# Norm tails, router and the lone expert unit of a two-block network: three edits in one change

## The chip, the cores and the metric

The kernel runs on one core of one Trainium2 chip. The time is device microseconds of one execution, as the median of several; one more execution was recorded by the hardware profiler, and every row below comes from that one.

## The reference, cut to what matters

256 tokens of width 1024 (`x`, two blocks of 128 tokens) pass through two layers of a first block and one layer of a second, all in float32.

```python
for l in range(2):                                  # first block
    x = layernorm(ALPHA * x + 0.5 * swiglu(x, ffn1))          # tail 1, 4
    x = layernorm(ALPHA * x + hybrid_mixer(x))                # tail 2, 5
    x = layernorm(ALPHA * x + 0.5 * swiglu(x, ffn2))          # tail 3, 6
h = rms_norm(x) * (1 + scale1) + shift1             # second block
x = x + gate1 * (concat(gated_deltanet(h), window_attention(h)) @ w_out)   # tail 7
h2 = rms_norm(x) * (1 + scale2) + shift2
# router: best of 4 groups, two experts of its 8, by softmax of h2 @ w_group, h2 @ w_router
for e in range(32):
    out += combine[:, e] * ((silu(h2 @ w_gate[e]) * (h2 @ w_up[e])) @ w_down[e])
x = x + gate2 * out
```

An expert is three matrices of 1024 x 256, 1024 x 256 and 256 x 1024.

## The kernel before, in words

**Products.** Dense weights are loaded as tiles of 128 x 1024, and `wload` makes of each a pair `hi` (a rounded copy, ScalarE, L304) and `lo` (the rest, VectorE, L305); the activations are kept as such a pair too, transposed, in `xhl`. Each product is then three matmuls. `execute` walks a list of items and loads up to two tiles ahead. A scheduler puts the instructions of each engine into an order when the kernel is built, by program order and priority; `keep_in_program_order` fixes an instruction's place, and each engine then runs its list in that order.

**A tail.** `outp` multiplies by an output matrix (w_out of a feed-forward part, w_mix_out, w_out_2), one tile of 128 rows after another, for both token blocks `tb`. The last four tiles are kept, and all their products for block 0 are done before those for block 1, so that the norm of block 0 (`finisher`'s `fn(0)`) runs beside the products of block 1. `fn` adds the residual (L500), takes mean and variance (L501, L503), the inverse root on GpSimd (L314), scales (L508, L509); `to_T` then transposes the block on TensorE (L331) and splits it into `xhl`. In the program, `to_T` of block 0 comes behind all products of block 1, and `to_T` of block 1 at the end of `fn(1)`. The next part starts with a leading product that does block 0 first, so that the norm of block 1 runs beside it; two of its four weight tiles go to spare buffers (`SPARE`). There are five such plain tails. In the sixth, ahead of the second block, `modnorm` follows with the second block's first norm: squares on ScalarE, an inverse root, then two VectorE passes over each half with gain and shift along rows (L1275, L1277).

**The router.** After `outp` by w_out_2, `fn` multiplies by the gate and adds (L1859, L1860), transposes the block (L1869, copies L1871), multiplies by the router's weights (L1873), and `tokens` makes a pair `th`, `tl` of the normed tokens (L1933, L1935), written so that the columns of one residue modulo 8 lie together. `route` then works out both experts of each token on VectorE. `moe` starts with eight products that put `x` into the output banks (L2257).

**The experts.** 32 experts in 16 pairs, up to 64 tokens each. For a pair: `gather` multiplies a 0/1 matrix by `th`, `tl` as weights (L2245: 256 products with a weight load of 128 columns each), `hidden` (L2085), `activate`, `turn` (L2103, L2107), `down` (L2122), `scatter` (L2141). The two experts of a pair sit in columns 0 to 63 and 64 to 127 of the array. One extra unit (`extra`, between the eighth and ninth pair) takes what one expert could not hold: 64 rows, one expert, so only columns 0 to 63. Weights of experts stream in meanwhile, through 14 large and 5 small buffers.

## Time and profile before

| | |
|---|---|
| median of 3 runs | 2105.73 us (2105.18 to 2108.71) |
| profiled execution, its own time | 2107.98 us |
| its span, first to last instruction | 2106.2 us |
| busy shares of the span | TensorE 98%, its weight loads 78%, VectorE 70%, ScalarE 52%, GpSimd 4% |
| chain that ended last | TensorE 86%, VectorE 8%, ScalarE 2% |
[...]
| moved by DMA | 427.60 MB, mean 203 GB/s |

A busy share says little by itself where it is an average over many stages; what an edit is worth is read from the stretch in which it lies. In the profile PE is TensorE's matmuls, PEld its weight loads, DVE VectorE, ACT ScalarE, POOL GpSimd; L331 is line 331 of the kernel before.

### The profile page before, as it was taken

The numbers are of one execution on the slowest core, as the hardware profiler recorded it, in microseconds if no ns is written. First come the engines' busy times: TensorE is split into PE (matmuls) and PEld (weight loads), VectorE is DVE, ScalarE is ACT, GpSimd is POOL, SyncE is SP. The second block draws the span as 40 slices with busy tenths as digits, with TensorE's granted clock in tenths as the row PEclk, the third lists the DMA queues.
The fourth block names the chain that finished last, engine by engine and source line by source line (L and its number), as shares of the span: only waits on it lengthen the run. The fifth ranks groups of instructions, "written<-read, shape, count | busy, mean of one in ns | idle before, by whom it ended". The sixth has DMA issues, their size and how long they took to land.

```text
span 2106.2 us, 30863 instructions
## 1 busy us (share of the span) xinstructions
PE 2057.2 (98%) x11507; PEld 1650.7 (78%) x11507; DVE 1470.6 (70%) x2782; ACT 1105.4 (52%) x2026; POOL 75.3 (4%) x64
## 2 busy tenths in 40 slices
PE   8999999999999999999999999999998999899998
PEld 7887877888888888888877888888887878645543
DVE  6886688987878677875688896877666675533333
ACT  5654565777655544554466776754553554322222
POOL 0000000100000000000000110000000121001000
PEclk9999999999999999999999999999999989999999
DMA  7985544454659676876544355565674423799996
GB/s 229 304 261 175 166 133 135 129 162 141 192 193 303 190 256 197 273 242 205 162 123 142 109 161 169 151 224 167 188 235 137 136 63 116 265 364 357 357 374 235
DMA packets 278825, 427.60 MB, mean 203 GB/s; under 512 B 21806, under 2 KB 206352, under 8 KB 277648
## 3 DMA queue, kind: packets, MB, share of 16 engines
q1 hardware_dynamic: 278240, 422.44, 61.6%
q0 software_dynamic: 432, 3.15, 0.4%
q8 instruction: 92, 1.51, 0.3%
q14 instruction: 61, 0.50, 0.1%
HBM read 424.46 MB, written 1.07 MB: 202 GB/s over the span
## 4 chain that ended last, share of the span: by engine, by line
PE 86%; DVE 8%; ACT 2%; issue 1%; POOL 1%; DMA 0%; SPq 0%; ACTq 0%; POOLq 0%; DVEq 0%
PE ps L408 27%; PE ps L411 14%; PE ps L2085 6%; PE y L342 5%; PE y L343 5%; PE y L345 4%; PE ps L2122 3%; PE ps L342 3%; PE ps L345 3%; PE ps L343 3%; DVE lo L305 2%; PE ps L2245 2%; PE y L2141 1%; PE y L331 1%; PE ps L301 1%
## 5 line engine op out<-in xcount | busy, mean ns | idle before, releaser
L305 DVE TENSOR_TENSOR lo<-raw,hi 128x1024 fp32r<-128x1024 f32 (+1 forms) x556 | 660.2, 1196 | 250.5 <-ACT hi L304 175.0
L304 ACT CAST hi<-raw 128x1024 fp32r<-128x1024 f32 (+1 forms) x556 | 556.6, 1028 | 337.5 <-PE y L345 169.6
L408 PE MATMUL ps<-xhl,hi 128*128 128x512 f32 x2240 | 568.4, 395 | 0.8 <-DVE kc L181 0.8
L408 PEld LDWEIGHTS ps<-xhl,hi 128*128 128x128 f32 x2240 | 402.1, 189 | 76.2 <-issue 3.3
L411 PEld LDWEIGHTS ps<-xhl,lo 128*128 128x128 f32 x2240 | 306.1, 190 | 21.7
L411 PE MATMUL ps<-xhl,lo 128*128 128x256 f32 x2240 | 314.7, 283 | 0.0
L342 PE MATMUL y<-hi,hh 128*128 128x512 f32 x352 | 137.3, 390 | 0.0
L343 PE MATMUL y<-lo,hh 128*128 128x512 f32 x352 | 137.0, 389 | 0.0
L342 PE MATMUL ps<-hi,xhl 128*128 128x512 f32 (+1 forms) x304 | 121.8, 402 | 3.5 <-DVE ra L803 2.2
L2085 PE MATMUL ps<-wgu,hi 128*64 128x512 f32 x512 | 121.1, 594 | 0.0
L345 PE MATMUL ps<-hi,xhl 128*128 128x512 f32 (+1 forms) x304 | 118.7, 393 | 1.9 <-DVE xhl L305 1.9
L343 PE MATMUL ps<-lo,xhl 128*128 128x512 f32 (+1 forms) x304 | 120.1, 395 | 0.0
L179 ACT ACTIVATE ysum<-ps 128x256 f32<-128x256 f32 x168 | 64.3, 383 | 77.4 <-PE ps L411 73.4
L345 PE MATMUL y<-hi,hl 128*128 128x512 f32 x352 | 104.5, 389 | 0.0
L2085 PEld LDWEIGHTS ps<-wgu,hi 128*64 128x64 f32 x512 | 42.6, 137 | 68.2 <-issue 64.7
L181 DVE TENSOR_TENSOR ysum<-ysum,ps 128x256 f32<-128x256 f32 x168 | 69.3, 415 | 29.0 <-ACT ysum L179 28.7
L342 PEld LDWEIGHTS y<-hi,hh 128*128 128x128 f32 x352 | 66.1, 188 | 14.8 <-issue 1.2
L345 PEld LDWEIGHTS y<-hi,hl 128*128 128x128 f32 x352 | 66.1, 188 | 13.7
L343 PEld LDWEIGHTS y<-lo,hh 128*128 128x128 f32 x352 | 66.1, 188 | 13.5
L342 PEld LDWEIGHTS ps<-hi,xhl 128*128 128x128 f32 x304 | 58.2, 192 | 19.4 <-ACT qs L795 3.0
L179 ACT ACTIVATE sg<-ps 128x256 f32<-128x256 f32 x80 | 30.4, 380 | 80.5 <-PE ps L411 80.4
L345 PEld LDWEIGHTS ps<-hi,xhl 128*128 128x128 f32 x304 | 58.1, 191 | 15.8 <-DVE xhl L305 4.3
(604 smaller groups left out, 3192.8 us busy)
## 6 DMA issues: line engine op xcount, KB each, us to landing
raw<-in_w_mix_in_dram SPq DMA_DIRECT2D x184, 512.0 KB
raw<-in_ffn_w_in_dram SPq DMA_DIRECT2D x176, 512.0 KB
raw<-in_ffn_w_out_dram SPq DMA_DIRECT2D x88, 512.0 KB
wgu<-in_w_gate_dram SPq DMA_DIRECT2D x64, 512.0 KB
wgu<-in_w_up_dram SPq DMA_DIRECT2D x64, 512.0 KB
lo<-in_w_down_dram SPq DMA_DIRECT2D x54, 512.0 KB
wada<-in_w_ada_dram SPq DMA_DIRECT2D x96, 256.0 KB
raw<-in_w_branch_dram SPq DMA_DIRECT2D x48, 512.0 KB
```

The source lines that it names most:

```text
L179: self.nc.scalar.activation(out, pb, AF.Copy, scale=scale)
L181: self.nc.vector.tensor_tensor(out, out, pa, op=ALU.add)
L304: self.nc.scalar.copy(hi, src)
L305: self.nc.vector.tensor_tensor(lo, src, hi.bitcast(F32), op=ALU.subtract)
L342: mm(y, ah[:, t], wh[:, c], start=start, stop=False)
L343: mm(y, ah[:, t], wl[:, c], start=False, stop=False)
L345: mm(y, al[:, t], wh[:, c], start=False, stop=stop)
L408: mm(ps.rearrange("p (a b) -> p a b", a=2), h[:, k % 4, c], xh.both(k), start=k == 0, stop=False)
L411: mm(ps[:, 0:256], l[:, k % 4, c], xh[:, k, :], start=False, stop=k == KD - 1)
L2085: mm(gu[64 * e:64 * e + 64, c], u["x"](k)[:, 64 * e:64 * e + 64], w, start=k == 0 and i == 0, stop=k == KD - 1 and i == len(ws[0]) - 1)
L2122: mm = lambda *a, **kw: self.placed(pin, self.nc.tensor.matmul(*a, **kw))
L2245: nc.tensor.matmul(ps[:, j, :], B["t"][tb][i][:, 128 * k:128 * k + 128], P[:, tb, :], start=n == 0, stop=n == 3)
```

## The change

- **Tails.** The last 6 tiles are kept in place of 4 (8 in the sixth tail), 2 or 4 of their pairs in large buffers; up to four tiles are loaded ahead of a spare one, and a third spare one is added. Block 1's products are done by halves of the columns, and `to_T` of block 0 is put into them (`mid`, ahead of item 18 of 24, or 24 of 32). `fn` and `to_T` are given a priority; `to_T` of block 1 is put right ahead of the leading product's part for block 1 (`late`). The transposes are fixed in program order.
- **Second block's norm (sixth tail).** Only the scale by the inverse root is done along rows; gain and shift come after the transposes, as columns (`modx`), and the load of their rows is dropped. The router's constants (`head`) are worked out here, not ahead of w_out_2.
- **Router.** The transposes of block 0 go ahead of the last four items of block 1's products; the order behind is: transposes of block 1's first half, router products of block 0, transposes of its second half, its router products. `tokens` writes in natural order, and the second parts `tl` are fixed in program order. `gather` takes its weights with a step of 8 elements (32 bytes).
- **Extra unit.** Gate in columns 0 to 63 and up in 64 to 127; for the output, column half 0 in the one and half 1 in the other; in `scatter`, half 0 from rows 0 to 63 and half 1 from rows 64 to 127.

```diff
-PRIO = {'narrow': 300, 'rope2': 300}
-
-SPARE, SPARE2 = (1, 2), (1,)
+PRIO = {'narrow': 300, 'rope2': 300, 'norm': 300}
+
+SPARE, SPARE2 = {1: "s2", 2: "s2", 3: "big"}, {1: "s2", 2: "s2", 3: "own"}
...
+TAIL, TAIL_BIG, MID = (6, 8), (2, 4), (18, 24)
...
-                while nxt < len(ws) and len(loaded) <= ahead:
+                while nxt < len(ws) and len(loaded) <= (4 if ws[nxt][5] else ahead):
...
-        if spare:
+        if spare == "big":
+            t = self.big.tile([128, 2048], F32R, name="wtail", tag="b8")
+            hi, lo = (t[:, i * 1024:i * 1024 + 1024] for i in range(2))
+            self.split(hi, lo, raw)
+            return (hi.rearrange("p (a b) -> p a b", a=a), lo.rearrange("p (a b) -> p a b", a=a))
+        if spare == "s2":
...
-        self.split(hi[:, :n], lo[:, :n], raw[:, :n])
+        last = self.split(hi[:, :n], lo[:, :n], raw[:, :n])
+        if self.pin:
+
+            self.tc.keep_in_program_order(last)
...
+                            if tb == NB - 1:
+                                self.late()
...
-            self.W(w[:, kn * j:kn * j + kn, c0:c0 + n], kn, n, tile(j), lead and j in spare)
...
-                        for part in ((0,), (1,)):
-                            for i, wt in enumerate(st["w"]):
-                                one(kt - last + i, wt, tb, part)
-                        fn(tb, st["ys"][tb])
+
+                        halves = [(0,), (1,)] if mid is not None and tb == NB - 1 else [(0, 1)]
+                        for n, (c, part, i) in enumerate((c, p, i) for c in halves for p in (0, 1) for i in range(last)):
+                            if len(halves) > 1 and n == mid[0]:
+                                mid[1]()
+
+                            one(kt - last + i, st["w"][i], tb, (part,), c, len(halves) > 1 and last == 4 and n >= mid[0])
+                        with self.tc.high_priority(prio) if prio else ExitStack():
+                            fn(tb, st["ys"][tb])
...
-            self.W(w[:, order[k]:order[k] + 1, :], 1, D, tile(k))
...
-                st["m"] = self.modrows(0, 1, "gain1")
                 st["h"] = self.t8([128, NB, D], F32, "h1")
+                self.B["head"] = self.head(self.B)
+                next(self.B["head"])
...
-            src = st["h"] if mod else st["x"]
-            if tb == NB - 1:
-                self.to_T(S_, src, 0)
...
-                h = st["h"][:, tb, :]
-                self.modnorm(st["x"][:, tb, :], st["m"], lambda n, t, s: (h[:, n * 512:n * 512 + 512], t, s))
+
+                x, h = st["x"][:, tb, :], st["h"][:, tb, :]
+                r = self.modnorm1(x, [h[:, 0:512], h[:, 512:1024]])[0][:, 0:1]
+                nc.scalar.activation(h[:, 0:512], x[:, 0:512], AF.Identity, scale=r)
+                nc.vector.tensor_scalar(h[:, 512:1024], x[:, 512:1024], r, None, op0=ALU.mult)
             if tb == NB - 1:
                 S_["x"] = st["x"]
-                self.to_T(S_, src, 1)
-        return pre, fn
-
-
-    def to_T(self, S_, x, tb):
+                self.late, self.pin = late, True
+
+        def mid():
+            with self.tc.high_priority(PRIO["norm"]):
+                self.to_T(S_, st["h"] if mod else st["x"], 0, mod)
+
+        def late():
+            self.pin = False
+            if mod:
+                next(self.B["head"])
+            with self.tc.high_priority(PRIO["norm"]):
+                self.to_T(S_, st["h"] if mod else st["x"], 1, mod)
+        return pre, fn, mid
...
-            pt = self.transposes(x[:, tb, j * 512:(j + 1) * 512])
+            pt = self.transposes(x[:, tb, j * 512:(j + 1) * 512], pin=True)
             o = (slice(None), slice(4 * j, 4 * j + 4), slice(tb * 128, tb * 128 + 128))
+            if mod:
+                y = self.sc([128, 4, 128], F32, "modx", True)
+                for k in range(4):
+                    shift, gain = (self.modc[:, i + 4 * j + k:i + 4 * j + k + 1] for i in (0, 8))
+                    if j:
+                        self.nc.vector.tensor_scalar(y[:, k, :], pt[:, k, :], gain, shift, op0=ALU.mult, op1=ALU.add)
+                    else:
+                        self.nc.scalar.activation(y[:, k, :], pt[:, k, :], AF.Identity, scale=gain, bias=shift)
+                pt = y
             self.split(xh[o], xl[o], pt)
-        if tb == NB - 1:
-            S_["xT"] = (xh, xl)
+        S_["xT"] = (xh, xl)
...
                     for tb in range(NB):
-                        ps = st["ps"][tb]
                         if not first:
+                            if tb == NB - 1:
+                                self.late()
                             for i in range(4):
                                 one(i, tb)
+                    for tb in range(NB):
...
+        self.outp(lambda k: (H[k // 8][0][:, k % 8, :], H[k // 8][1][:, k % 8, :]), wout, KF, fn, last=TAIL[mod], pre=pre,
+                  big=TAIL_BIG[mod], mid=(MID[mod], mid), prio=PRIO["norm"])
...
         self.JOIN("swa")
-        self.DO(lambda: (B.update(pj=True), B["head"]()))
+        self.DO(lambda: (B.update(pj=True), next(B["head"], None)))
...
+        hT = {}
+
+        def turned(tb, j, pin=False):
+            pt = self.bank([128, 4, 128], pj=True)
+            for k in range(4):
+                t = nc.tensor.transpose(pt[:, k, :], S_["x"][:, tb, (4 * j + k) * 128:(4 * j + k + 1) * 128], self.ident)
+                if pin:
+                    self.tc.keep_in_program_order(t)
+            hT[tb, j] = self.sc([128, 4, 128], F32, "xT2")
+            nc.scalar.copy(hT[tb, j], pt)
+
+        def logits(tb, j):
+            for k in range(4 * j, 4 * j + 4):
+                nc.tensor.matmul(B["pr"][:, tb, :], hT[tb, j][:, k % 4, :], B["wr"][:, k, :], start=k == 0, stop=k == KD - 1)
+
+
+        def mid():
+            B["pr"] = self.bank([128, 2, 36], pj=True)
+            for j in range(2):
+                turned(0, j, True)
...
             if tb == 0:
-                B["pr"] = self.bank([128, 2, 36], pj=True)
+                nrm = self.modnorm1(x)
+                B["rs"].append(nrm[0][:, 0:1])
+                self.tokens(B, x, nrm[0][:, 0:1])
+                return
+            turned(1, 0)
+            logits(0, 0)
+            logits(0, 1)
+            turned(1, 1)
+            logits(1, 0)
+            logits(1, 1)
+
+            B["lo"][0]()
             nrm = self.modnorm1(x)
             B["rs"].append(nrm[0][:, 0:1])
-            hT = []
-            for j in range(2):
-                pt = self.bank([128, 4, 128], pj=True)
-                for k in range(4):
-                    nc.tensor.transpose(pt[:, k, :], x[:, (4 * j + k) * 128:(4 * j + k + 1) * 128], self.ident)
-                hT.append(self.sc([128, 4, 128], F32, "xT2"))
-                nc.scalar.copy(hT[j], pt)
-            for k in range(KD):
-                nc.tensor.matmul(B["pr"][:, tb, :], hT[k // 4][:, k % 4, :], B["wr"][:, k, :], start=k == 0, stop=k == KD - 1)
             self.tokens(B, x, nrm[0][:, 0:1])
-            if tb == 0:
-                B["lo"][0]()
-        return pre, fn, head
+        return pre, fn, mid
...
+        yield
+        ps = self.bank([128, 36], pj=True)
+        for k in range(KD):
+            self.tc.keep_in_program_order(nc.tensor.matmul(ps, self.modc[:, 24 + k:25 + k].to_broadcast([128, 128]), wr[:, k, :],
+                                                           start=k == 0, stop=k == KD - 1))
...
+        B["wr"] = self.hi_p.tile([128, 1024], F32, name="hi", tag="hi")[:, 0:KD * 36].rearrange("p (k n) -> p k n", k=KD)
+        nc.vector.tensor_tensor(B["wr"], wr, self.modc[:, 32:40].rearrange("p (k o) -> p k o", o=1).to_broadcast([128, KD, 36]), op=ALU.mult)
+        B["rs"], B["t"], B["lo"] = [], [], []
...
-        to = lambda a: a.rearrange("p (k q) -> p q k", k=KD)
-        xv = x.rearrange("p (q k) -> p q k", k=KD)
-        nc.scalar.activation(to(th), xv, AF.Identity, scale=r)
+        nc.scalar.activation(th, x, AF.Identity, scale=r)
         B["t"].append((th, tl))
-        B["lo"].append(lambda: nc.vector.scalar_tensor_tensor(to(tl), xv, r, to(th).bitcast(F32), op0=ALU.mult, op1=ALU.subtract))
+        B["lo"].append(lambda: self.tc.keep_in_program_order(
+            nc.vector.scalar_tensor_tensor(tl, x, r, th.bitcast(F32), op0=ALU.mult, op1=ALU.subtract)))
...
+            if u.get("alone"):
+
+                for i, (_, w) in enumerate(ws[0]):
+                    mm(gu[64 * i:64 * i + 64, 0:256], u["x"](k)[:, 0:64], w, start=k == 0, stop=k == KD - 1)
+                continue
...
+        if u.get("alone"):
+            nc.scalar.activation(h[0:64, :], gu[0:64, 0:256], AF.Silu)
+            nc.vector.tensor_copy(h[64:128, :], gu[64:128, 0:256])
+            u["h"] = h
+            return
...
-        nc.scalar.copy(u["hT"][:, :, 0:m], pt[:, 0:2, 0:m])
+        if u.get("alone"):
+            hT = u["hT"][:, :, 0:64]
+            nc.scalar.copy(hT, pt[:, 0:2, 0:64])
+            nc.vector.tensor_tensor(hT, hT, pt[:, 0:2, 64:128], op=ALU.mult)
...
+        if u.get("alone"):
+
+            y = self.bank([128, 512], pj=True)
+            yg, yh, yl = (self.sc([128, 512], dt, i) for dt, i in ((F32, "yg"), (F32R, "yh"), (F32R, "yl")))
+            for k in range(2):
+                for n in range(2):
+                    mm(y[64 * n:64 * n + 64, :], u["hT"][:, k, 0:64], u["wd"][0][k][:, n * 512:n * 512 + 512], start=k == 0, stop=k == 1)
+            for n in range(2):
+                q = slice(64 * n, 64 * n + 64)
+                self.nc.vector.scalar_tensor_tensor(yg[q, :], y[q, :], u["w"][q, :], B["gt"][q, 1, n * 512:n * 512 + 512], op0=ALU.mult, op1=ALU.mult)
+            self.split(yh, yl, yg)
+            u["y"] = [(yh, yl)] * 2
+            return
...
+        if u.get("alone"):
+            for tb in range(NB):
+                for i in range(2):
+                    for n in ns:
+                        q = slice(64 * n, 64 * n + 64)
+                        mm(ys[tb][n], u["PT"][q, tb, :], u["y"][n][i][q, :], start=start and i == 0, stop=stop and i == 1)
+            return
...
+        u["alone"] = m == 64
+        if u["alone"]:
+
+            for t in range(NB):
+                nc.vector.tensor_copy(Po[t][:, :, 64:128], Po[t][:, :, 0:64].bitcast(F32))
+        u["Pw"] = lambda tb: Po[tb][:, 2, 0:128 if u["alone"] else m].bitcast(F32)
...
-                nc.vector.tensor_copy(xs[n][0:m, :], ps[0:m, :])
+
+                for j in range(2):
+                    nc.vector.tensor_copy(xs[j].rearrange("s (k p) -> s k p", k=4)[0:m, :, 64 * n:64 * n + 64],
+                                          ps[0:m, :].rearrange("s (p k) -> s k p", k=KD)[:, 4 * j:4 * j + 4, :])
...
-                    nc.tensor.matmul(ps[:, j, :], B["t"][tb][i][:, 128 * k:128 * k + 128], P[:, tb, :], start=n == 0, stop=n == 3)
+                    nc.tensor.matmul(ps[:, j, :], B["t"][tb][i][:, k:D:KD], P[:, tb, :], start=n == 0, stop=n == 3)
```

## Rows read from the trace of the kernel before

**Rows 1.** Busy time by stretch: tails 1 and 5, tail 6, router; from the last product on.

```profile
core 0: us, PE busy (x) PEld busy (x) DVE busy (x) ACT busy (x) POOL busy (x), PEclk, DMA share, GB/s
200.30:216.20 15.90, 14.45 (x69) 10.75 (x67) 13.72 (x22) 6.58 (x9) 1.00 (x1) 1.00 0.47 135
...
1430.30:1447.00 16.70, 15.08 (x117) 13.66 (x116) 13.96 (x21) 7.86 (x12) 1.00 (x1) 1.00 0.45 129
1618.70:1637.10 18.40, 11.80 (x42) 8.50 (x41) 16.86 (x38) 7.14 (x16) 2.02 (x3) 0.72 0.40 120
1818.50:1838.80 20.30, 15.90 (x78) 11.57 (x76) 13.34 (x53) 8.26 (x13) 0.56 (x1) 0.75 0.76 285
```

**Rows 2.** Timeline, tail 1, TensorE: start, us, what, idle before and who ended it.

```profile
201.74 0.50 PE L342 MATMUL ps<-hi,xhl 128*128 128x512 f32 x1 [0.33 <-ACT xhl L304]
...
207.23 0.39 PE L343 MATMUL ps<-lo,xhl 128*128 128x512 f32 x1
...
207.46 0.40 PE L345 MATMUL ps<-hi,xhl 128*128 128x512 f32 x1
...
208.64 1.32 PE L331 MATMUL y<-ctab,x 128*128 128x128 f32 x8 [0.78 <-DVE x L509]
...
211.03 0.50 PE L345 MATMUL ps<-hi,xhl 128*128 128x512 f32 x1 [0.33 <-DVE xhl L305]
```

**Rows 3.** Timeline, tail 1, VectorE: first and last step of block 0's norm.

```profile
194.90 1.28 DVE L500 SCALAR_TENSOR_TENSOR x<-x,y 128x512 f32<-128x512 f32 x2 [1.88 <-PE y L345]
...
199.05 1.41 DVE L509 SCALAR_TENSOR_TENSOR x<-x,rs,lngb 128x512 f32<-128x512 f32 x2
```

**Rows 4.** Timeline, tail 6: the modulated norm and its transposes.

```profile
1621.42 1.42 DVE L1275 SCALAR_TENSOR_TENSOR mn<-x,ssm,gain 128x512 f32<-128x512 f32 x2
1622.76 1.29 DVE L1277 TENSOR_TENSOR h<-mn,gain 128x512 f32<-128x512 f32 x2
...
1623.50 1.97 PE L331 MATMUL y<-ctab,h 128*128 128x128 f32 x8 [4.60 <-DVE h L1277]
...
1635.71 1.26 PE L331 MATMUL y<-ctab,h 128*128 128x128 f32 x8 [0.72 <-DVE h L1277]
```

**Rows 5.** Timeline of the router, TensorE.

```profile
1819.84 1.98 PE L1873 MATMUL ps<-hi,xT 128*128 128x36 f32 x16 [0.29 <-ACT xT L1871]
...
1824.98 1.09 PE L1869 MATMUL ps<-ctab,x 128*128 128x128 f32 x4 [2.70 <-DVE x L1860]
1826.11 3.63 PE L1873 MATMUL ps<-hi,xT 128*128 128x36 f32 x16
...
1836.79 2.12 PE L2245 MATMUL ps<-P,raw 128*128 128x256 f32 x16 [0.90 <-DVE P L2220]
```

**Rows 6.** Timeline of the router, VectorE: the second part of block 1's tokens.

```profile
1830.56 1.97 DVE L1935 SCALAR_TENSOR_TENSOR raw<-x,ssm,raw 128x1024 fp32r<-128x1024 f32 x1
```

**Rows 7.** Groups by line and form, experts (1838 to 2100 us): busy, mean ns | idle.

```profile
L2085 PE MATMUL ps<-wgu,hi 128*64 128x512 f32 x512 | 121.1, 594 | 0.0
...
L2085 PEld LDWEIGHTS ps<-wgu,hi 128*64 128x64 f32 x512 | 42.6, 137 | 68.2 <-issue 64.7 <-DVE yg L2130 1.7 <-DVE hi L2207 0.3
L2245 PE MATMUL ps<-P,raw 128*128 128x256 f32 x248 | 33.7, 286 | 0.0
L2245 PEld LDWEIGHTS ps<-P,raw 128*128 128x128 f32 x246 | 30.3, 188 | 3.7 <-issue 2.4 <-DVE yg L2130 1.2
...
L2085 PE MATMUL ps<-wrow,hi 128*64 128x256 f32 x32 | 7.1, 379 | 0.0
...
L2122 PE MATMUL ps<-wrow,hT 128*64 128x512 f32 x8 | 3.6, 598 | 0.0
...
L2141 PE MATMUL y<-yh,PT 64*128 64x512 f32 x4 | 1.7, 416 | 0.0
```

**Rows 8.** Single lines: duration ns min/median/max, first and last start, forms.

```profile
L1933 ACT ACTIVATE raw<-x,ssm x2: 2052/2067/2082, 1820.2 to 1826.6; 128x1024 fp32r<-128x1024 f32 x2
...
L304 ACT CAST hi<-raw x556: 292/1049/1102, 9.4 to 1801.8; 128x1024 fp32r<-128x1024 f32 x176, 128x512 fp32r<-128x512 f32 x9, 128x128 fp32r<-128x128 f32 x1
...
L2107 PEld LDWEIGHTS y<-ctab,hs x34: 195/200/220, 1857.7 to 2090.0; 128*128 128x128 f32 x32, 64*128 64x128 f32 x2
```

**Rows 9.** Busy time by stretch, experts; columns as in the first group.

```profile
2000.00:2010.00 10.00, 10.00 (x49) 3.19 (x46) 2.79 (x4) 1.24 (x2) 0.00 (x0) 1.00 0.68 201
2030.00:2040.00 10.00, 10.00 (x51) 3.48 (x48) 2.87 (x5) 1.23 (x2) 0.00 (x0) 1.00 1.03 409
```

More of the change, by code (lines that the diff above doesn't have):

```diff
@@ L339, in mm_tok @@
             for j, y in enumerate(ys):
+                if j not in cols:
+                    continue
                 c = slice(j * 512, min(j * 512 + 512, wh.shape[1]))
@@ L378, in tok @@
         for j in range(parts):
-            self.W(w[:, kn * j:kn * j + kn, c0:c0 + n], kn, n, tile(j), lead and j in spare)
+            self.W(w[:, kn * j:kn * j + kn, c0:c0 + n], kn, n, tile(j), lead and spare.get(j))
     def fm(self, xT, w, c0, fn, wide=True):
@@ L437, in narrow, with outp, one @@
         self.W(w[:, :, c0:c0 + 16], KD, 16, run)
-    def outp(self, aT, w, kt, fn, last=4, pre=None, order=None, join={}, pre_at=None, tail=None):
+    def outp(self, aT, w, kt, fn, last=4, pre=None, order=None, join={}, pre_at=None, tail=None, big=0, mid=None, prio=0):
         st = {}
         order = order or range(kt)
-        def one(k, wt, tb, parts=(0, 1)):
+        def one(k, wt, tb, parts=(0, 1), cols=(0, 1), pin=False):
             ah, al = aT(order[k])
-            self.mm_tok(st["ys"][tb], tb, ah, al, wt[0][:, 0, :], wt[1][:, 0, :], k == 0, k == kt - 1, parts)
+            self.mm_tok(st["ys"][tb], tb, ah, al, wt[0][:, 0, :], wt[1][:, 0, :], k == 0, k == kt - 1, parts, cols, pin)
         def tile(k):
@@ L474, in outp @@
                 self.JOIN(join[k])
-            self.W(w[:, order[k]:order[k] + 1, :], 1, D, tile(k))
+            self.W(w[:, order[k]:order[k] + 1, :], 1, D, tile(k), "big" if 0 <= k - (kt - last) < big else None)
     def finisher(self, S_, g, b, mod=False):
@@ L568, in run @@
                     for tb in range(NB):
[L569 removed]
                         if not first:
+                            if tb == NB - 1:
+                                self.late()
                             for i in range(4):
                                 one(i, tb)
+                    for tb in range(NB):
+                        ps = st["ps"][tb]
                         sg = self.sc([128, 256], F32, "sg", True)
[L574 removed]
+                        a = nc.scalar.activation(sg, ps[:, 0:256], AF.Silu)
+                        if tb == 0 and not first:
+                            self.tc.keep_in_program_order(a)
                         nc.vector.scalar_tensor_tensor(sg, sg, 0.5, ps[:, 256:512], op0=ALU.mult, op1=ALU.mult)
@@ L589, in lead @@
                 c0 = (j // 2) * D_FF
-                self.W(win[:, 4 * (j % 2):4 * (j % 2) + 4, c0:c0 + 256], 4, 256, tile(j), not first and j in SPARE)
+                self.W(win[:, 4 * (j % 2):4 * (j % 2) + 4, c0:c0 + 256], 4, 256, tile(j), not first and SPARE.get(j))
         def pair(f):
@@ L785, in mixer @@
         wo = I["w_mix_out"][l].rearrange("(k p) n -> p k n", p=128)
-        pre, fn = self.finisher(S_, I["ln2_g"][l], I["ln2_b"][l])
-        self.outp(lambda k: (L["m"][0][:, k, :], L["m"][1][:, k, :]), wo, KD, fn, pre=pre)
+        pre, fn, mid = self.finisher(S_, I["ln2_g"][l], I["ln2_b"][l])
+        self.outp(lambda k: (L["m"][0][:, k, :], L["m"][1][:, k, :]), wo, KD, fn, last=TAIL[0], pre=pre, big=TAIL_BIG[0],
+                  mid=(MID[0], mid), prio=PRIO["norm"])
     def rotate(self, L, name, n, ps):
@@ L1253, in modrows, with modnorm1 @@
         return t
-    def modnorm(self, x, G, out):
-        self.modnorm2(x, G, out, self.modnorm1(x))
-    def modnorm1(self, x):
+    def modnorm1(self, x, t=None):
         nc = self.nc
         ss = self.small.tile([128, 2], F32, name="ssm", tag="ssm")
-        t = [self.sc([128, 512], F32, "mn") for _ in range(2)]
+        t = t or [self.sc([128, 512], F32, "mn") for _ in range(2)]
         for n in range(2):
@@ L1268, in modnorm1 @@
         return ss, t
-    def modnorm2(self, x, G, out, st):
-        nc = self.nc
-        ss, t = st
-        for n in range(2):
-            c = slice(n * 512, n * 512 + 512)
-            nc.vector.scalar_tensor_tensor(t[n], x[:, c], ss[:, 0:1], G[:, 1, c], op0=ALU.mult, op1=ALU.mult)
-            o, i0, i1 = out(n, t[n], G[:, 0, c])
-            nc.vector.tensor_tensor(o, i0, i1, op=ALU.add)
     def block2(self, S_, us):
@@ L2098, in turn @@
         nc = self.nc
-        m = u["m"]
+        m = 128 if u.get("alone") else u["m"]
         pt = self.bank([128, 4, 128])
```

55 lines of the change are left out of this document (28 added, 27 removed).

## The prediction

> **What bounds the kernel now.** I read the busy shares first: TensorE works in 98% of a span of 2106.2 us, so all that the change can win is idle time of TensorE, columns that its array handles, or clock. The chain that ended last says the same (86% TensorE, 8% VectorE, 2% ScalarE), and its VectorE part sits in the norms and the router. So I went to the stretches around them [rows 1]. In tail 1 TensorE is busy for 14.45 of 15.90 us, in tail 5 for 15.08 of 16.70: 1.45 and 1.62 us lost, the clock full. Tail 6 loses 6.6 of 18.40 us with a mean granted clock of 0.72, the router 4.4 of 20.30 us at 0.75; these two alone lose clock as well.
>
> The timeline shows where a plain tail loses its 1.5 us [rows 2]: 0.33 us ahead of a product that waits for ScalarE's half of `xhl`, 0.78 us ahead of block 0's transposes (for the norm's last step, L509), 0.33 us ahead of the first leading product, which waits for the split (L305). In the experts TensorE has no idle time in either stretch, and DMA still has slack in one (0.68 of its engines at 201 GB/s, where 409 GB/s were moved in the other) [rows 9]. There only fewer or cheaper columns help.
>
> The sum goes against the profiled execution: 2107.98 us, its span and 1.8 us around it. That is 2.25 us above the median of 2105.73, so I take 2.25 off at the end. About 0.2% (4.2 us) is what this measurement can tell from no change.
>
> **Five plain tails.** Block 0's norm takes from 194.90 to 199.05 + 1.41 us, 5.6 us [rows 3]. Today 4 tiles x 6 = 24 products of block 1 cover it, at the 0.23 us between neighbours [rows 2] 5.5 us. With six tiles block 1 has 36 products and the transposes go in behind item 18 of 24. Items with the rounded half of the activations have two matmuls, the others one, so 12 x 2 + 6 x 1 = 30 of the 36 stand ahead: 30 x 0.23 = 6.9 us. That covers 5.6 with 1.3 to spare, and the 6 matmuls behind (1.4 us) cover the cast and split, so the 0.78 and one 0.33 go. In the leading part `late` puts block 1's transposes ahead of block 1's products, so a short wait for the transposed block may stay there: bounds -0.7 us (one gap goes) and -2.4 us (all idle, and the work behind it starts earlier on ScalarE and VectorE). I take -1.5, near what the rows lose: 5 x -1.5 = **-7.5**. What is covered stays so only while the weight splits of the next tiles do not stand ahead of the norm on VectorE; if they do, the gap comes back (rival C). The two extra kept tiles sit in large buffers, their loads go out two earlier on SP, and DMA is at 0.40 to 0.47 here [rows 1], so I cost these at nothing.
>
> **Tail 6.** Block 0's transposes wait 4.60 us for L1277, then both sets of 8 take 1.97 and 1.26 us [rows 4]. The norm is longer by two VectorE passes over each half, 1.42 and 1.29 us [rows 4]; these fall away, and 8 smaller steps per block take their place behind the transposes, on the way from bank to `xhl`. With eight tiles 24 of 32 items stand ahead, 16 x 2 + 8 x 1 = 40 matmuls x 0.23 = 9.2 us ahead of the transposes, where the modulated norm now needs about 5.6 plus squares, root and scale (2 to 3): covered. Of 18.40 us, useful work at full clock is 24 matmuls x 0.23 = 5.5 and 16 transposes at 1.26/8 = 0.16, 2.5: 8.0, so 10.4 us are lost between waits and clock. What stays is a wait for block 1's norm, with the new column steps in front of its split: 3 us, -7.5. Bounds: -10 (clock and waits all won) and -5 (the wait for L1277 alone). The eight products of the router's constants move here from a stretch without idle time, which I cost at nothing. **-7.5**.
>
> **Router.** [...] The second wait goes when block 0's transposes and products stand behind it as work: -2.7; the clock, if kept, -1.65; L1933 takes 2.07 us against 1.05 of a contiguous pass of the same shape [rows 8], twice, one of them ahead of work that waits: -1. L1935 (1.97 us, [rows 6]) leaves the routing chain but must be done before the first gather, and comes back behind `places`: -0.8 net. Sum **-6.2**; bounds -4 (clock not kept, the pass hidden) and -9 (4.4 us idle and all the clock).
>
> **Extra unit.** Products on one half of the array cost 7.1 us for 32 x 256 columns, 0.222 each; pairs cost 0.237 for 512 columns [rows 7], so 256 columns of two halves side by side cost 0.119: 3.8 us, -3.3. `down` likewise from 3.6 to 8 x 0.237 = 1.9: -1.7. `scatter` has 1.7 us in 4 with 64 rows; if its row halves run side by side it saves 0.9, if not 0: -0.4. Its transposes take 128 columns in place of 64: +0.2. **-5.2**, bounds -4.5 and -6.2.
>
> **Gather with a step.** The price here is not in the trace. 256 weight loads (248 and 246 of them in the stretch of [rows 7], with some records missing) now pick every eighth element of `th`, `tl`. The load takes 188 ns and the gather's matmuls 33.7/248 = 0.136 us each, so a longer load shows at once: nothing else covers it. Below nothing is excluded, as the load moves as many elements. Above, three rows:
> - L2107 loads 128 columns with a step of 8 bytes in 200 ns against 188 [rows 7, 8]: 12 ns, 256 x 12 = 3 us.
> - If the load's column rate halved: (188 - 137)/64 = 0.80 ns per column [rows 7], 128 x 0.80 = 102 ns, 26 us.
> - ScalarE's pass took 2067 ns written with a step of 512 bytes, 1049 contiguous [rows 8]: 0.99 ns an element, 127 ns, 32.5 us.
>
> L2107 is the nearest in kind (a weight load, with a step), and a moving pass takes 0.23 us for 512 columns, 0.45 ns each, where the load takes 0.80: its reading has room for a slower memory. I take **+3**, ends 0 and +32.5.
>
> ScalarE's row shows that a step can double a pass. [...]
>
> **Sum.** -7.5 - 7.5 - 6.2 - 5.2 = -26.4; +3 gives -23.4. 2107.98 - 23.4 = 2084.6; less 2.25, **2082** as a median. Adding bounds as independent, its own range is 2075 to 2091.
>
> **Rivals.**
> - **A, slower: each strided load pays what ScalarE's pass pays.** Place: L2245's successor in all 16 pairs. +32.5 - 26.4 = +6.1: 2111.8 (2107 to 2116). For it: [rows 8], and no slack in the gather. Against: L2107, and the load's low rate. It decides from 26.4 us/256 = 103 ns a load on.
> - **A', same: the load's rate halves.** +26.1, or +22 where the matmul hides part: 2101 to 2105.4.
> - **C: the tails give half.** VectorE is busy 13.72 of 15.90 and 16.86 of 18.40 us in them [rows 1]; if splits and the new column steps stand ahead of the norm, plain tails and tail 6 give -7 together in place of -15: 2082.3 + 8 = 2090, and with half the router lost too 2093.
> - **D: transfers.** In one stretch the DMA engines were full [rows 9]. With 5.2 us less work the weights behind the extra unit must come earlier; if they do not, -5.2 is lost: 2087.5.
> - **E: the change does not do what it says**: the two halves of the extra unit do not run side by side. Then -5 is lost: 2087.5. [rows 7] speak against it, as pairs do.
>
> **How the numbers follow.** My forecast .48; A .20; A' .14; C .11; D .04; E .03. Faster: .48 + .11 + .04 + .03 = .66, less .02 for a mix of C with part of the price that ends within 0.2%, and A' counts .01 here (2101): .65. Same: A' .13, that .02, and .02 of A's lower end: .17. Slower, the rest of A: .18. The range has to reach to A's centre, as .20 lie there: 2074 to 2113, which leaves out A's upper part (.06) and the ends of the forecast (.05).
>
> **What would show it.**
> - L2245's successor: weight load near 200 ns and 16 matmuls near 1.9 us a pair mean my term; 290 to 315 ns and a pair longer by 1.6 to 2 us mean A or A'. This step carries most of the doubt, and alone can put the result on the other side.
> - Plain tails: TensorE's idle time falls from 1.5 to a few tenths, and the transposes of block 0 stand inside block 1's products with no wait. If a wait for L509's successor stands there, C.
> - Tail 6: granted clock near 1.0, one wait of 2 to 3 us at block 1's norm.
> - Router: no 2.70 us wait; its second 16 products near 2 us; last dense product to first gather 6 us sooner.
> - Extra unit: its 32 and 8 products busy 3.8 and 1.9 us, against 7.1 and 3.6.
> - Wrong beyond these: a wait of the first gather on `tl`, or DMA waits in the pairs behind the extra unit.

## The result: slower, by the gather's weight loads

The changed kernel takes 2125.56 us (median of 5 runs, 2121.52 to 2126.24) against 2107.75 us (5 runs, 2105.18 to 2111.35): ratio 1.008, interval 1.0065 to 1.0096. The forecast was 2082 us; the range ended at 2113. The profiled execution spans 2123.8 us against 2106.2, 17.6 us more.

Where they go is read by equal places of the program in both profiles. The first gather starts at 1836.79 us before [rows 5] and at 1829.33 after, 7.5 us earlier. From there to the end it was 269.4 us and is 294.5: 25.1 us later. So all that is lost is lost among the experts. Groups by line and form of the changed kernel, experts, TensorE (columns as in [rows 7]):

```profile
L2155 PE MATMUL ps<-wgu,hi 128*64 128x512 f32 x512 | 121.2, 594 | 0.0
L2354 PE MATMUL ps<-P,raw 128*128 128x256 f32 x256 | 65.8, 408 | 0.9 <-DVE P L2329 0.9
...
L2150 PE MATMUL ps<-wrow,hi 128*64 128x256 f32 x32 | 3.6, 379 | 0.0
...
L2202 PE MATMUL ps<-wrow,hT 128*64 128x512 f32 x8 | 1.9, 605 | 0.0
...
L2234 PE MATMUL y<-yh,PT 64*128 64x512 f32 x4 | 0.9, 443 | 0.0
```

The gather's group in the kernel before, over the same stretch:

```profile
L2245 PE MATMUL ps<-P,raw 128*128 128x256 f32 x256 | 34.7, 286 | 0.9 <-DVE P L2220 0.9
```

The pairs' products (L2155) cost what they did. The gather (L2354) went from 34.7 us for its 256 matmuls to 65.8: **+31.1 us**. The extra unit (L2150, L2202, and the halves of L2234) went from 7.1 + 3.6 us [rows 7] to 3.6 + 1.9, and its scatter from 1.7 to 0.9 in each of two groups: about -7. What the gather spends is the time of its weight loads (single line: duration ns min/median/max, first and last start):

```profile
L2354 PEld LDWEIGHTS ps<-P,raw x256: 312/337/343, 1829.3 to 2074.9; 128*128 128x128 f32 x128
```

A load takes 337 ns where it took 188 [rows 7], and the matmuls show no other wait than the 0.9 us ahead of the first, which stood there before. 149 ns more a load, 31.1 us/256 = 121 ns of them in the time; the other 28 do not show in it. What the step was to pay for came too: the tokens' pass on ScalarE fell from 2067 ns [rows 8] to 1154 (L1997).

The stretches that answer to [rows 1], busy time by stretch (columns as there): tails 1 and 5, tail 6, router:

```profile
198.70:214.60 15.90, 15.35 (x73) 11.85 (x72) 12.53 (x20) 7.79 (x10) 0.99 (x1) 1.00 0.47 137
1427.10:1443.80 16.70, 15.19 (x110) 14.62 (x110) 12.12 (x18) 7.91 (x11) 1.00 (x1) 0.90 0.51 158
1613.20:1635.00 21.80, 18.00 (x74) 14.00 (x73) 14.78 (x37) 11.08 (x23) 2.39 (x2) 0.77 0.29 97
1812.00:1829.33 17.33, 14.88 (x72) 11.03 (x71) 9.37 (x45) 6.16 (x14) 1.11 (x2) 0.80 0.91 332
```

In tail 1 TensorE now loses 0.55 us in place of 1.45; tail 5 loses 1.5 (1.6 before), at a granted clock of 0.90; tail 6 still loses 3.8 of its now longer stretch at 0.77, and in the router the clock is 0.80, where it was 0.75.

### The profile page after: what moved, and what is told of

Same layout as the page of the kernel before. It is cut to its first block, busy times and chain, and to the rows that moved or that the text cites. A ratio compares the mean times of both kernels' runs of the same rounds, so it can differ in the third digit from the quotient of the medians.

```text
span 2123.8 us, 30878 instructions
## 1 busy us (share of the span) xinstructions
PE 2080.4 (98%) x11507; PEld 1681.0 (79%) x11507; DVE 1468.8 (69%) x2789; ACT 1110.5 (52%) x2036; POOL 76.1 (4%) x64
## 4 chain that ended last, share of the span: by engine, by line
PE 88%; DVE 7%; ACT 2%; issue 1%; POOL 1%; DMA 0%; SPq 0%; ACTq 0%; POOLq 0%; DVEq 0%
PE ps L427 27%; PE y L351 14%; PE ps L430 14%; PE ps L351 8%; PE ps L2155 5%; PE ps L2354 3%; PE ps L2202 3%; DVE lo L317 2%; PE y L2234 1%; PE y L343 1%; PE ps L313 1%; PE ps L312 1%; PE ps L311 1%; DVE cv L1010 1%; PE y L1117 1%
## 5 line engine op out<-in xcount | busy, mean ns | idle before, releaser
L317 DVE TENSOR_TENSOR lo<-raw,hi 128x1024 fp32r<-128x1024 f32 (+2 forms) x538 | 637.2, 1192 | 220.3 <-ACT hi L316 140.3
L316 ACT CAST hi<-raw 128x1024 fp32r<-128x1024 f32 (+2 forms) x538 | 536.4, 1026 | 259.2 <-PE y L351 81.6
L351 PE MATMUL ps<-hi,xhl 128*128 128x512 f32 (+1 forms) x592 | 190.7, 396 | 5.5 <-DVE ra L856 2.2
L351 PE MATMUL y<-lo,hh 128*128 128x512 f32 x312 | 121.5, 389 | 0.0
L351 PE MATMUL y<-hi,hh 128*128 128x512 f32 x312 | 121.4, 389 | 0.0
L2155 PE MATMUL ps<-wgu,hi 128*64 128x512 f32 x512 | 121.2, 594 | 0.0
L2155 PEld LDWEIGHTS ps<-wgu,hi 128*64 128x64 f32 x512 | 42.5, 137 | 68.2 <-issue 65.6
L351 PE MATMUL y<-hi,hl 128*128 128x512 f32 x312 | 92.9, 389 | 0.0
L351 PEld LDWEIGHTS y<-hi,hl 128*128 128x128 f32 x312 | 58.6, 188 | 12.3
L351 PEld LDWEIGHTS y<-lo,hh 128*128 128x128 f32 x312 | 58.6, 188 | 12.1
L351 PEld LDWEIGHTS ps<-lo,xhl 128*128 128x128 f32 x296 | 56.6, 191 | 14.4 <-DVE lo L317 2.9
L2354 PE MATMUL ps<-P,raw 128*128 128x256 f32 x256 | 65.8, 408 | 0.9 <-DVE P L2329 0.9
```

The lines of the kernel that those rows point to most:

```text
L316: self.nc.scalar.copy(hi, src)
L317: return self.nc.vector.tensor_tensor(lo, src, hi.bitcast(F32), op=ALU.subtract)
L351: mm = lambda *a, **kw: self.placed(pin, self.nc.tensor.matmul(*a, **kw))
L2155: mm(gu[64 * e:64 * e + 64, c], u["x"](k)[:, 64 * e:64 * e + 64], w, start=k == 0 and i == 0, stop=k == KD - 1 and i == len(ws[0]) - 1)
L2354: nc.tensor.matmul(ps[:, j, :], B["t"][tb][i][:, k:D:KD], P[:, tb, :], start=n == 0, stop=n == 3)
```

## The experiments

Two theories stood against each other. **S**: the step in the weights is the whole loss, and without it the change is worth what the rest of the forecast said. **Rival**: the rest is also worth less than forecast. Each was right in part: the step is the whole loss, and the rest is worth less than forecast. The versions are compared with the kernel before by ratio; a label stands for one kernel.

**contig**: the changed kernel with the tokens by residue again.

```diff
-        nc.scalar.activation(th, x, AF.Identity, scale=r)
+        nc.scalar.activation(to(th), xv, AF.Identity, scale=r)
...
-                    nc.tensor.matmul(ps[:, j, :], B["t"][tb][i][:, k:D:KD], P[:, tb, :], start=n == 0, stop=n == 3)
+                    nc.tensor.matmul(ps[:, j, :], B["t"][tb][i][:, 128 * k:128 * k + 128], P[:, tb, :], start=n == 0, stop=n == 3)
```

The second parts on VectorE and the copy behind the extra unit's gather change along with it.

> The changed kernel with tokens written by residue again and the gather's weights contiguous; all else of the change stays. Theory S (the step is the whole loss): the 256 gather matmuls fall from 65.8 us busy back to 34.7 and their loads from 337 to 188 ns; of the 31 us that come back up to 1 us goes to ScalarE's slower pass with a step in the router, so 2094 to 2096 us, 0.993 to 0.994 of the kernel before. Rival (the pairs are late for another reason as well, transfers or the new order): the matmuls fall, but other waits take part of it, and the time ends at 2100 or above.

Measured: 2097.88 us, 0.9955 (0.9942 to 0.9969), the gather at 34.9 us. The loss turns into a gain of 9.5 us by the ratio, and this version beats both kernels; but its time lies 2 us above what theory S gave and 2 below the rival, and the gain is far from the 26.4 that the forecast had without the step. One piece of it is a wait of the gather for the tokens' second part, 1.22 us (timeline, TensorE):

```profile
1829.08 0.94 PE L2353 MATMUL ps<-P,raw 128*128 128x256 f32 x6 [0.90 <-DVE P L2328]
1831.24 1.45 PE L2353 MATMUL ps<-P,raw 128*128 128x256 f32 x10 [1.22 <-DVE raw L2002]
```

**step_alone**: the kernel before with the step alone (the reverse of that diff).

> The kernel before with the step alone (tokens in natural order, gather's weights with a step of 8 elements, the extra unit's gather sorted on its way out of the bank). Theory S: +31 us in the gather, up to 2 us won in the router by the contiguous passes (1049 ns in place of 2067, twice), 2135 to 2139 us, ratio 1.013 to 1.015. Rival (the step costs so much only beside the other edits): below 2125 us.

Measured: 2136.54 us, 1.0138 (1.0123 to 1.0154): +29 us by the ratio, in a kernel that has none of the other edits. That the step is the whole loss holds from both sides.

**steps**: a ruler. Each k gathers with a step of k + 1 elements of 4 bytes.

```diff
-                    nc.tensor.matmul(ps[:, j, :], B["t"][tb][i][:, k:D:KD], P[:, tb, :], start=n == 0, stop=n == 3)
+                    t, o = B["t"][tb][i], dict(start=n == 0, stop=n == 3)
+                    if k == 0:
+                        nc.tensor.matmul(ps[:, j, :], t[:, 0:128], P[:, tb, :], **o)
+                    elif k == 1:
+                        nc.tensor.matmul(ps[:, j, :], t[:, 0:256:2], P[:, tb, :], **o)
...
+                    elif k == 7:
+                        nc.tensor.matmul(ps[:, j, :], t[:, 0:1024:8], P[:, tb, :], **o)
```

> A ruler for the load: the changed kernel, in which the eight gathers k = 0 to 7 take weights with a step of 1, 2, 3, 4, 5, 6, 7 and 8 elements from the token's start. It gathers the wrong columns, so only durations count. Theory line (a second read from the same 16 bytes is cheap, a new line costs): steps 1 to 3 near 188 to 200 ns, 4 to 8 all near 337. Rival slope (the cost grows with the bytes that are passed): 188 ns at 1 and 337 at 8 with some 21 ns a step between. Rival doubling: every step above 1 near 337. TensorE's gather time between 34.7 and 65.8 us accordingly.

Single lines, steps 1 to 8 in order:

```profile
L2356 PEld LDWEIGHTS ps<-P,raw x32: 186/189/201, 1829.9 to 2046.3; 128*128 128x128 f32 x32
```
```profile
L2358 PEld LDWEIGHTS ps<-P,raw x32: 192/194/200, 1831.5 to 2046.8; 128*128 128x128 f32 x32
```
```profile
L2360 PEld LDWEIGHTS ps<-P,raw x32: 251/261/263, 1830.2 to 2047.4; 128*128 128x128 f32 x32
```
```profile
L2362 PEld LDWEIGHTS ps<-P,raw x32: 318/329/332, 1832.2 to 2048.3; 128*128 128x128 f32 x32
```
```profile
L2364 PEld LDWEIGHTS ps<-P,raw x32: 296/322/328, 1835.2 to 2062.1; 128*128 128x128 f32 x32
```
```profile
L2366 PEld LDWEIGHTS ps<-P,raw x32: 317/321/326, 1836.1 to 2063.0; 128*128 128x128 f32 x32
```
```profile
L2368 PEld LDWEIGHTS ps<-P,raw x32: 305/329/332, 1839.1 to 2064.0; 128*128 128x128 f32 x32
```
```profile
L2370 PEld LDWEIGHTS ps<-P,raw x32: 334/338/341, 1840.0 to 2064.9; 128*128 128x128 f32 x32
```

No slope (5 to 8 lie between 321 and 338) and no jump at 2: the theory of the line, but for step 3, which was put with the cheap ones and lies half-way. A count by groups of 16 bytes fits these times: at step 2 every group that is touched gives two elements, from step 4 on one. (329 - 189)/128 = 1.09 ns more, then, for an element that is alone in its group. At step 3, of four elements two share a group and two are alone, so 64 are alone: 189 + 64 x 1.09 = 259 ns; measured 261. At a lower clock a load took as long: one of a single repeated column took 333 ns in tail 6 of the changed kernel (L1935), where 0.50 was granted, and 190 in the kernel before (L1848), where it was 1.00. But that is not behind the steps: over the gathers of this version, 1830 to 2066 us, the granted clock is 1.00.

**extra_alone**: the kernel before with the extra unit's edits alone.

> The kernel before with the extra unit's edits alone. The changed kernel's rows show its products at 3.6 + 1.9 + 1.7 us where the kernel before had 7.1 + 3.6 + 3.3, so theory P (what the rows save comes off the end): -5 to -7 us, 2099 to 2101, ratio 0.9967 to 0.9975. Rival D (transfers: the expert weights can't come earlier, DMA at 0.94 to 1.0 of its engines there): -3 us or less, 2103 and above.

Measured: 2101.09 us, 0.9977 (0.9968 to 0.9986), -4.8 us by the ratio. That is just short of theory P's -5, and more than rival D left.

**tails_alone** and **router_alone**: the kernel before with one group of edits each, the gather contiguous.

> The kernel before with the edits of the tails and of the second block's norm alone (router order, tokens and extra unit as before). Theory M (read from the two profiles by equal places in the program: -1.3, -0.3, -1.3, -1.2, +0.5 us in the five plain tails, -0.3 in tail 6 and -0.3 where the router's constants left): -3 to -5 us, 2101 to 2103. Rival (the tails give the 15 us that their idle time promises, and something later takes it): -10 us or more, 2096 and below.

> The kernel before with the router's order alone (block 0's transposes among block 1's products, products of each half as its transposes come, second parts of the tokens fixed in order), tokens by residue and the gather contiguous. Theory M (the profile of the changed kernel: 3.2 us less up to the first gather, of which the contiguous version gives 1.2 back in a wait for the tokens' second part): -1 to -3 us, 2103 to 2105. Rival (the predicted -6.2): 2100 to 2101.

Measured: 0.9991 (0.9982 to 1.0), -1.9 us, and 1.0004 (0.9995 to 1.0013), nothing. So most of the 15 and 6.2 us of the forecast was not there to be taken away later; it never came. Theory M expected too much as well, -3 to -5 and -1 to -3. The router alone shows where its gain went: the wait of 2.70 us [rows 5] fell to 1.48, but one of 1.15 for the routing (`onehot`, 0.45 before) and a new one of 1.23 for the tokens' second part stand behind it. tails_alone keeps one edit of the router's group, the fixed place of that second part. Its profile stands 5.7 us ahead of the kernel before behind tail 6 (at 1700 us), 2.7 at the router, and 0.35 at the end. 3.0 us go ahead of w_out_2, where the constants left and where the clock differs between executions (last section); 2.3 go at the first gather, which waits 1.22 us for the second part, and in the first pairs. So the tails' edits won more than the -1.9 shows, and lost it behind them.

The rest asks why the tails give so little, on the contiguous version. **prio0**: priority for block 0's norm alone.

```diff
-   with self.tc.high_priority(prio) if prio else ExitStack():
+   with self.tc.high_priority(prio) if prio and tb == 0 else ExitStack():
```

> The contiguous version with the priority for the norm of block 0 alone; block 1's norm is ordered among the weight splits as before. Theory V (block 1's norm, put first, holds up the splits of the next weights on VectorE): the 2.41 us wait for a second weight part in tail 6 and the 1.27 us wait in tail 5 go, 2 to 5 us below the contiguous version. Rival (block 1's norm is itself what is late): waits of 0.4 to 0.8 us for its last step come back in the five plain tails, 0 to 4 us above it.

Measured: 0.9964 (0.9951 to 0.9978), not to be told from 0.9955. The 2.41 us wait for a weight's second part in tail 6 became one of 4.03 for the norm; the plain tails kept their waits to within some 0.2. The priority of block 1's norm does not set them.

**nopin**: the line that fixes weight splits in program order, `self.pin = True`, left out.

> The contiguous version without fixing the weight splits between block 1's norm and its transposes in program order. Theory O (the fixed order puts up to three splits, 3.49 us, ahead of block 1's own split in tail 5): the 1.46 us wait there and the 1.41 us wait in tail 2 shrink, 1 to 3 us below the contiguous version. Rival (VectorE simply has that much work there): waits move, within 1 us.

Measured: 0.9962 (0.9948 to 0.9976). Tail 5's wait of 1.46 is now 1.22 + 0.56, tail 2's went from 1.41 + 0.56 to 1.20 + 0.56: not the fixed order.

**nolo**: leading tiles 1 to 3 without a second part.

```diff
+        if spare and a > 1:
+            if spare == "s2":
...
+                return Rows(hi, b), Same(self.zero.to_broadcast([128, b]))
```

> The contiguous version without the second parts of the leading weight tiles 1 to 3 behind each tail (their products are done with a zero column in its place, so the work of TensorE stays). Theory V (splits of the next weights on VectorE stand in the way of block 1's norm): the waits of 5.3 us in the five plain tails and the 2.41 us in tail 6 mostly go, 5 to 8 us below the contiguous version. Rival N (block 1's norm, transposes and split are by themselves longer than the 5.5 to 5.7 us of leading products): 2 us or less, with waits for the last norm step still there.

Measured: 0.9949 (0.9935 to 0.9962), no difference from contig. But it does not speak against theory V in the plain tails: in tail 2 splits of other tiles moved into the same three places ahead of block 1's norm, and the wait was 1.31. In tail 6 the 2.41 us became 2.71 for the norm itself.

**nolo_all**: no second part for any dense tile.

> The contiguous version with no second part of any dense weight tile worked out on VectorE (products with a zero column in its place, so TensorE's work stays; the experts have none). Some 640 us of VectorE's work go. Theory V (splits stand in front of block 1's norm and of its own split): waits in the five plain tails fall from 5.3 us to 1.5 or less, 4 to 8 us below the contiguous version. Rival N (block 1's norm, transposes, cast and split are by themselves longer than the leading products): 3 us of them stay, 3 us or less below.

Measured: 2052.84 us, 0.9742 (0.9729 to 0.9756), far more than either theory. Most of it is not the tails: TensorE's busy time fell from contig's 2049.3 to 2021.5 us for the same 11507 instructions, as products with a zero column ran a little faster (`lo` by `hh`, 389 ns on the mean, 378 with zero), so its time is no measure of the tails. Its waits are: all that the timeline shows in the plain tails sum to 5.56 us in contig and to 1.75 here, none over 0.29 and none for the norm. Tail 2, where the changed kernel's TensorE waits 1.20 us, on VectorE: timeline of the changed kernel and of this one:

```profile
631.74 1.32 PE L343 MATMUL y<-ctab,x 128*128 128x128 f32 x8 [1.20 <-DVE x L532]
```
```profile
624.89 0.68 DVE L523 SCALAR_TENSOR_TENSOR x<-x,y 128x512 f32<-128x512 f32 x1
625.49 1.22 DVE L317 TENSOR_TENSOR lo<-raw,hi 128x1024 fp32r<-128x1024 f32 x1
626.62 0.69 DVE L524 BATCH_NORM_STATS2 st<-x 128x6 f32<-128x512 f32 x1
627.23 1.21 DVE L317 TENSOR_TENSOR lo<-raw,hi 128x1024 fp32r<-128x1024 f32 x1
628.35 0.20 DVE L526 BATCH_NORM_AGGREGATE mv<-st 128x2 f32<-128x12 f32 x1
628.47 1.17 DVE L317 TENSOR_TENSOR lo<-raw,hi 128x1024 fp32r<-128x1024 f32 x1
...
629.62 1.40 DVE L531 SCALAR_TENSOR_TENSOR x<-x,mv,lngb 128x512 f32<-128x512 f32 x2
630.95 1.41 DVE L532 SCALAR_TENSOR_TENSOR x<-x,rs,lngb 128x512 f32<-128x512 f32 x2
```
```profile
610.46 0.69 DVE L527 SCALAR_TENSOR_TENSOR x<-x,y 128x512 f32<-128x512 f32 x1
611.18 0.69 DVE L528 BATCH_NORM_STATS2 st<-x 128x6 f32<-128x512 f32 x1
611.91 0.21 DVE L530 BATCH_NORM_AGGREGATE mv<-st 128x2 f32<-128x12 f32 x1
...
612.23 1.41 DVE L535 SCALAR_TENSOR_TENSOR x<-x,mv,lngb 128x512 f32<-128x512 f32 x2
613.55 1.41 DVE L536 SCALAR_TENSOR_TENSOR x<-x,rs,lngb 128x512 f32<-128x512 f32 x2
```

With the splits (L317), block 1's norm takes from 624.89 to 632.36, 7.5 us, of which three splits are 3.6; without them 4.5 us. 5.7 us of leading products cover 4.5 and not 7.5. Theory V holds for the plain tails, with a little more left than the 1.5 us that it allowed. In tail 6, 1.99 for the norm and 1.40 for the cast stay: there rival N holds.

**pool**: those splits on GpSimd. They also lose their fixed order, and all four leading tiles are loaded up to four ahead, so that this version does not change the engine alone.

```diff
-            self.split(hi, lo, raw)
+            self.split(hi, lo, raw, self.nc.gpsimd if a > 1 else None)
...
+        self.split(hi[:, :n], lo[:, :n], raw[:, :n], self.nc.gpsimd if self.pin or spare else None)
```

> The contiguous version, in which GpSimd works out the second parts of the leading weight tiles behind each tail (all four, and those loaded while block 1's norm is under way) in place of VectorE; the tiles' look-ahead is as for a spare one. Theory V: VectorE's row loses 3 to 4 splits of 1.2 us in front of block 1's norm and of its own split, the waits of 5.3 us in the plain tails fall to some 2 us, 2 to 5 us below the contiguous version. Rival G (GpSimd is too slow: it took 1290 ns for 128 x 512 elements in the kernel before, so some 2.6 us for a tile): TensorE waits for second parts by GpSimd in place of that, at or above the contiguous version.

Measured: 2124.77 us, 1.0091 (1.0078 to 1.0105), so 27 us above contig's median. In the plain tails TensorE doesn't wait for GpSimd, as rival G had it, but still for VectorE, some 3 us a tail, 16.4 in sum for contig's 5.6; where the rest of the 27 us goes was not followed. Tail 2, VectorE and GpSimd:

```profile
622.69 1.41 DVE L528 SCALAR_TENSOR_TENSOR x<-x,mv,lngb 128x512 f32<-128x512 f32 x2
...
628.56 0.70 DVE L521 BATCH_NORM_STATS2 st<-x 128x6 f32<-128x512 f32 x1
...
629.61 4.20 DVE L528 SCALAR_TENSOR_TENSOR x<-x,mv,lngb 128x512 f32<-128x512 f32 x2
634.26 1.42 DVE L529 SCALAR_TENSOR_TENSOR x<-x,rs,lngb 128x512 f32<-128x512 f32 x2 [0.45 <-POOL rs L323]
```
```profile
628.03 5.23 POOL L314 TENSOR_TENSOR lo<-raw,hi 128x1024 fp32r<-128x1024 f32 x2 [4.19 <-ACT hi L313]
633.23 1.00 POOL L323 TENSOR_TENSOR rs<-rs,mhalf 128x1 f32<-128x1 f32 x1
```

The two norm passes of L528, 1.41 us for block 0 at 622.69, take 4.20 for block 1 at 629.61, beside two splits on GpSimd of 5.23 together (3.33 to 4.50 in the five tails), and the inverse root queues behind those splits. Not every pass is slowed: L521 takes its 0.70 us beside the same splits. That GpSimd's work slows these passes is read from their places in time; no version takes it apart.

**head_back**: the router constants' products back ahead of w_out_2.

> The contiguous version with the products of the router's constants back ahead of w_out_2. Theory H (in tail 6 they cost 3.47 us at half clock, and they left waits of 0.43 and 0.76 us behind where they were): 1 to 3 us below the contiguous version, whose median was 0.9955 of the kernel before. Rival (they filled a wait for block 1's norm in tail 6, which now shows as idle time): within 1 us of it or above.

Measured: 0.9956 (0.9943 to 0.997), the rival: without them tail 6 shows a wait of 1.00 us for the norm where they stood (there they took 3.47 us; back ahead of w_out_2 they take 1.97).

## Why the prediction was wrong

- **Gather with a step: the step that failed, and the whole of the sign.** "L2107 is the nearest in kind ... I take +3": +31.1 us. L2107 is a weight load with a step, but with 8 bytes, two elements to each 16 bytes; the edit has 32. What mattered, by the run steps, was not the kind of instruction but whether each 16 bytes that are touched give two elements (194 ns) or one (329), and the row with a step past that, ScalarE's [rows 8], was at hand: its 127 ns a load met the measured 121. The argument that a load's low rate of 0.80 ns per column leaves room was wrong too: an element alone in its 16 bytes added 1.09 ns to it (steps). Rival A had the place and the price (+32.5), and 0.20. That its 127 ns meet the 121 so well is in part luck: the loads grew by 149, and the forecast that nothing covers a longer load missed the 28 that do not show. Its time of 2111.8 was too low too, as it took over the 26.4 us of the other terms.
- **Plain tails: -7.5, came -3.6 in the profiles.** (-1.3, -0.3, -1.3, -1.2, +0.5.) The cover for block 0 worked: the wait ahead of block 0's first leading product, 0.33 to 0.38 a tail, is gone in all five. But I read the 0.78 us at L331 [rows 2] as block 0's transposes, and the last 0.33 as the first leading product's. Both are block 1's: 24 leading products stand between 201.74 us and the 0.78. Block 0's transposes stand ahead of them and did not wait (timeline of the kernel before):

```profile
200.38 1.04 PE L331 MATMUL y<-ctab,x 128*128 128x128 f32 x8
```

  The edit gives block 1 no more cover, and its norm stays behind splits on VectorE (rival C's mechanism, by nolo_all). In tail 2 that wait rose from 0.44 to 1.20.
- **Tail 6: -7.5, came -0.3.** Block 0's 4.60 us [rows 4] went, as forecast, and the waits in sum fell from 6.5 to 3.8 us. The term left out what is late next. Timeline of the changed kernel, TensorE:

```profile
1623.60 0.50 PE L351 MATMUL ps<-lo,xhl 128*128 128x512 f32 x1 [2.41 <-DVE lo L317]
...
1625.14 3.47 PE L1935 MATMUL ps<-wr,mod 128*128 128x36 f32 x16
1628.42 1.95 PE L343 MATMUL y<-ctab,h 128*128 128x128 f32 x8
1631.76 0.80 PE L351 MATMUL ps<-hi,xhl 128*128 128x512 f32 x1 [1.39 <-ACT xhl L316]
```
```profile
1624.00:1633.00 9.00, 7.61 (x33) 6.56 (x32) 5.23 (x10) 3.93 (x8) 1.43 (x1) 0.53 0.71 234
```

  2.41 us for a weight's second part that stands behind block 1's norm on VectorE; then a low clock (0.53 granted from 1624 to 1633 us, behind that idle time: block 1's eight transposes take 1.95 us at 0.50, block 0's took 1.04 at 1.00), and the router's constants, costed at nothing, take 3.47 us of it, at 0.50. Moving either wait only brings the other (prio0, nolo, head_back): block 1's norm, with squares, root and scale, is what is late. And where the constants left, waits of 0.43 and 0.76 opened.
- **Router: -6.2, came -3.2, and nothing alone.** The 2.70 us wait became 1.47, not 0. The term has block 0's transposes and products stand as work in this wait, but the edit puts block 0's 16 router products (1.87 us at 1817.20) behind the transposes of block 1's first half in TensorE's order. ScalarE had their inputs, the copies of block 0's transposes, done at 1815.06; TensorE stood from 1815.26 to 1816.73. So they covered nothing of it; no run puts them ahead. The -1.65 for the clock is 3.63 less 1.98 us, the second and the first 16 products of [rows 5], which ran at granted clocks of 0.50 and 1.00; the edit did not win it: the second 16 still take 3.47 us, at 0.50. Timeline of the changed kernel, ScalarE and TensorE:

```profile
1813.99 1.07 ACT L1889 COPY xT<-ps 128x512 f32<-128x512 f32 x2 [1.79 <-PE ps L1885]
```
```profile
1816.73 0.63 PE L1885 MATMUL ps<-ctab,x 128*128 128x128 f32 x4 [1.47 <-DVE x L1907]
1817.20 1.87 PE L1893 MATMUL ps<-hi,xT 128*128 128x36 f32 x16
...
1819.64 3.47 PE L1893 MATMUL ps<-hi,xT 128*128 128x36 f32 x16
...
1829.33 0.97 PE L2354 MATMUL ps<-P,raw 128*128 128x256 f32 x3 [0.90 <-DVE P L2329]
```

  That the parts do not add up (0.9991 x 1.0004 x 0.9977 x 1.0138 = 1.011 against 1.008) is partly this: only with tokens in natural order is their second part, 1.28 us in place of 2.00, ready for the gather; tails_alone and router_alone each hold that wait, of 1.22 and 1.23 us. How much of the difference that is stays open, at the width of these intervals.
- **Extra unit: -5.2, came -4.8.** Right, for a slightly different sum: scatter's row halves do run side by side (3.3 to 1.7 us), and what the rows gained beyond that did not reach the end.

## What to carry to other kernels

Cost a weight load with a step by how many elements it takes from each 16 bytes (194 ns at two, 329 at one, in steps), and look for a row with as large a step, on whatever engine, before the nearest instruction: ScalarE's 0.99 ns an element [rows 8] came near the loads' 1.09. 256 loads in a stretch without cover made a question of nanoseconds one of 31 us. Before a wait is put down to a part, count the products ahead of it and say whose it is; cover given to one half of a two-block pipeline leaves the other half's wait where it was. Put the work that is to cover a wait ahead of the waiting instruction in its engine's order: block 0's router products stood behind it, had their inputs at 1815.06 us and began at 1817.20. And read the clock with the rows of a piece that is moved: the router's constants took 3.47 us at a granted clock of 0.50, in place of 1.97.

## What the runs showed of the hardware

- Weight loads of 128 columns of 4 bytes took 189, 194, 261, 329 ns at steps of 1 to 4 elements, 321 to 338 beyond (steps); 190 for one repeated column at a granted clock of 1.00 (kernel before, L1848), 333 at 0.50 (changed kernel, L1935).
- Beside GpSimd's splits two VectorE passes of L528 over 128 x 512 took 4.20 us in place of 1.41, one of L521 its 0.70 as ever (pool). GpSimd's subtraction of 128 x 1024 took 2.4 to 2.7 us in the tails (pool).
- The clock of the same stretch differed between executions of like kernels. Ahead of w_out_2, windows of the kernel before, extra_alone and nolo:

```profile
1737.50:1750.00 12.50, 12.50 (x83) 10.77 (x84) 6.28 (x19) 6.22 (x17) 2.51 (x2) 0.86 0.37 124
```
```profile
1734.85:1747.00 12.15, 12.15 (x94) 10.67 (x95) 7.45 (x23) 7.43 (x19) 2.87 (x3) 1.00 0.36 131
```
```profile
1727.11:1740.00 12.89, 12.67 (x62) 11.24 (x62) 5.07 (x14) 4.23 (x12) 2.52 (x2) 0.60 0.24 83
```

  0.86, 1.00 and 0.60, with TensorE busy in all but a fraction; all three begin behind the same wait, of 1.87, 1.60 and 1.89 us. From the first to the third group of the products that begin them (L1675; L1738 in nolo) 12.21, 10.60 and 14.66 us pass: 1.6 us between the first two, where no edit touches the stretch, and up to 4.1 with nolo, from which the constants' products have even left it. Terms of a few us that are read from two single profiles are no surer than that where the clock is below 1.00: tail 6 and the router above all.
